# An encoder trunk on one core: the gates of two branches as seven block products ahead of attention, and two weight sums from adding transfers

## The chip, the cores and the metric

The kernel runs on one core of a Trainium2 chip. The metric is the device time of one execution in microseconds, as the median of several runs; lower is better. A profile of one execution gives, for each engine, which instruction ran when and what it waited for. The engines are PE (TensorE, the matrix engine; PEld is its loading of weights), DVE (VectorE), ACT (ScalarE), POOL (GpSimd) and SP (SyncE, which here issues transfers and computes nothing). Each engine works through its own list of instructions strictly in order.

## The reference

Two layers of an encoder on 512 tokens of width 1024, in float32. Cut to what matters:

```python
x = layer_norm(x, ln_in_g, ln_in_b)
for l in range(2):
    proj = x @ w_in[l]                       # 1024 -> 6816
    na_q, na_k, na_v, df_q, df_k, df_v, m_cq, m_ckv, m_kr, gate_pre = split(proj)
    na_out  = neighbourhood_attention(na_q, na_k, na_v, rpb)          # 8 heads of 64
    df_out  = diff_attention(df_q, df_k, df_v, lam, subln_g)          # 4 heads of 2 x 64
    mla_out = latent_attention(m_cq, m_ckv, m_kr, w_qb, w_kvb, ...)   # 8 heads
    gates   = sigmoid(gate_pre + b_gate[l])                           # 3 branches x 1024
    merged  = sum(gates[:, b] * (o_b @ w_branch[l, b]) for b, o_b in ((0, na_out), (1, df_out), (2, mla_out)))
    x = layer_norm(ALPHA * x + merged @ w_out[l], ln1)
    gu = x @ w_ffn_in[l]                     # 1024 -> 2 x 2816
    x = layer_norm(ALPHA * x + (silu(gu[:, :2816]) * gu[:, 2816:]) @ w_ffn_out[l], ln2)
```

A differential head has two score matrices, takes a softmax of each, mixes the two with the factor lam, multiplies by the values, and normalizes the result by its root mean square.

## The kernel before

**Precision and tiles.** Every float32 operand is held as two parts, a rounded one (hi) and the remainder (lo), both in a format that PE reads fast. A product is three matmuls: hi x hi, hi x lo, lo x hi (`mm3`, and in `gemm_w` and `gemm_x` lines 156 to 158). A weight tile is loaded into a slot and split by `wsplit`: ACT copies it into `whi` (L138), DVE subtracts (`wlo`, L139). The transposed input lies in `xth` and `xtl`, 8 blocks of 128 channels x 512 tokens. Other splits go through `split` (ACT in L221, DVE in L222; L224 and L225 with a scale).

**Memory.** `H` is a pool of 8 slots of 128 x 1024 float32, `R` one of 38 slots of 128 x 512 hi or lo values. Weight loads use two `raw` buffers and four each for `whi` and `wlo`. PSUM, where matmuls write, has two banks under each of the names `acc`, `sc`, `pv` and `tr`.

**A layer.** First the values of neighbourhood attention (`na_values`) and the latents (`latents`: 672 columns in two halves of 336, then norms and transposes). Then 4 pairs of heads of neighbourhood attention (`na_pair`), 4 pairs of latent attention (`mla_pair`), 4 differential heads (`df_proj`, `df_head`; L476 and L477 are its scores, L478 the maximum, L481 to L483 the mixing of the two softmaxes, L486 the transposes, L491 and L492 the values, L495 to L503 the norm and transposing of the result). The output projection and the FFN follow.

**Gates and merges.** A gate step, `gates(l, b, mp, ...)`, makes 256 channels of branch `b`'s gate: two products of 8 x 3 matmuls of 512 columns, and Tanh, since sigmoid(x) = (1 + tanh(x/2))/2. A merge step multiplies a branch's projected output by its gate and adds it up. Which of these steps are written after which head is a table, `PLAN`: rows 0 to 3 after the pairs of neighbourhood attention, rows 4 to 7 after those of latent attention, rows 8 to 11 after the differential heads, row 12 last. `G21g` is gate step `mp` = 1 of branch 2, put into buffers `gt`; with `h` it lies in a slot of `H`; `M21` is its merge. The program is written in that order, and a scheduler then orders each engine's instructions: it takes those that are ready by its own reckoning of time, so that the matmuls of gates and merges come to lie between those of the heads.

**Block products.** In the FFN two of 11 sets of 256 gate and 256 up columns are computed plainly, the other 9 by `ffn_fast`. It cuts the weights into four blocks (top and bottom half of the 1024 channels, gate and up columns) and the input into four (channel halves `kh`, token halves `th`), and gets the four results from seven products of blocks rather than eight, with sums of weight blocks and sums of input blocks (`x_sums`, once per layer, eight `R` slot pairs). One product (`product`, L784) is 24 matmuls of 256 columns. The weight sums are formed on DVE, in place in `H` slots (L844 to L846, and one later on g1); a set loads four blocks of 512 KB.

All transfers of weights, inputs and copies are issued on SP's queue, in order.

Of the kernel before, what the change touches and what calls it, by code (L numbers as in the profile page):

```python
# [16 lines left out]
D = 1024  # L17
# [19 lines left out]
    "G20h",  # L37
# [8 lines left out]
    "",  # L46
# [35 lines left out]
def trunk(ctx, tc, x, ln_in, w_in, feat, bias, lamv, w_mla, w_mlr, w_mlv, w_branch, w_out,  # L82
# [23 lines left out]
    xd = [xs.tile([128, D], F32, name=f"xd{t}") for t in range(NT)]  # L106

# [401 lines left out]
    def latents(l, g):  # L509
        lat = [H.get() for _ in range(NT)]  # L510
        krs = [i[:, 672:800] for i in lat]
        for i in krs:
            G.memset(i, 0.0)
        for hf in range(2):
            c0 = C_LAT + hf * 336
            src = lambda a, b: [w_in[l, a:b, c0:c0 + 336]]
            ch = wload_ks(src, 336, (3, 3, 2))
            for t in range(NT):
                p = bank("acc")[:, :336]
                gemm_x(p, ch, slice(0, 336), XT, tsl(t), KD)  # L520
                A.activation(lat[t][:, hf * 336:(hf + 1) * 336], p, AF.Copy)
        for t in range(NT):
            for a, b in ((0, 384), (384, 640)):
                ss = stat()
                sq = ptile()
                A.activation(sq[:, :b - a], lat[t][:, a:b], AF.Square, scale=(b - a) ** -0.5, accum_out=ss)
                rpow(ss, ss, RMS_EPS)
                V.tensor_scalar(lat[t][:, a:b], lat[t][:, a:b], ss, None, op0=OP.mult)
            t1 = sp.tile([128, 32], F32, tag="kr1", name="kr1", bufs=2)
            t2 = sp.tile([128, 32], F32, tag="kr2", name="kr2", bufs=2)  # L530
            kr = lat[t][:, 640:672]
            V.tensor_mul(t1, kr, cosm[:, t])
            V.tensor_mul(t2[:, 0:16], kr[:, 16:32], sinm[:, t, 0:16])
            V.tensor_mul(t2[:, 16:32], kr[:, 0:16], sinm[:, t, 16:32])
            V.tensor_add(krs[t][:, 32:64], t1, t2)
            V.tensor_copy(krs[t][:, 64:96], krs[t][:, 32:64])
# [201 lines left out]
    def x_sums():  # L738
# [5 lines left out]
        for i in range(2):  # L744
# [9 lines left out]
            V.tensor_sub(t1, q(h(0, 1)), q(h(0, 0)))  # L754
            V.tensor_sub(d, q(lo(0, 1)), q(lo(0, 0)))
            V.tensor_add(t1, t1, d)
            V.tensor_sub(t2, q(h(1, 1)), t1)
            V.tensor_add(t2, t2, q(lo(1, 1)))
            halves(1, ts[1])
            halves(0, ts[0])  # L760
            V.tensor_sub(d, t2, q(h(0, 0)))
            V.tensor_sub(d, d, q(lo(0, 0)))
            halves(2, ts[2])
            V.tensor_sub(t1, q(h(1, 0)), t2)
            V.tensor_add(t1, t1, q(lo(1, 0)))
# [21 lines left out]
    def hidden(gate, up):  # L787
# [3 lines left out]
        V.tensor_mul(sg, sg, up)  # L791
# [31 lines left out]
    def ffn_fast(l, m, sums):  # L823


        def load(t, base, kh):
            c = slice(base + m * 128, base + (m + 2) * 128)
            nc.sync.dma_start(t.rearrange("p (k c) -> p k c", k=4),
                              w_ffn_in[l, kh * 512:(kh + 1) * 512, c].rearrange("(k p) c -> p k c", p=128))
            return t  # L830
# [4 lines left out]
        g0, u0, u1 = load(H.get(), 0, 0), load(H.get(), D_FF, 0), load(H.get(), D_FF, 1)  # L835
        s = H.get()
        g1 = load(wp.tile([128, 1024], F32, tag="raw", name="raw", bufs=2), 0, 1)
# [4 lines left out]
        t1, t2, t3, t4 = sums  # L842
        with tc.high_priority():
            V.tensor_add(s, u0, u1)  # L844
            V.tensor_sub(u0, g0, u0)
            V.tensor_sub(g0, s, g0)  # L846
# [9 lines left out]
        with tc.high_priority():  # L856
            V.tensor_sub(g1, g1, g0)
# [4 lines left out]
        H.put(s, u0, g0, u1)  # L862
        res = [hidden(px, p1)]
        res.append(hidden(u2, u3))
        return res

# [23 lines left out]
    for l in range(DEPTH):  # L890
# [19 lines left out]
        tiles, cq, ckv, kr = latents(l, fp[:, 25:30])  # L910
# [3 lines left out]
        def fill(steps):  # L914

            for kind, b, mp, *place in steps:
                b, mp, place = int(b), int(mp), "".join(place)
                if kind == "G":
# [12 lines left out]
                    gates(l, b, mp, bg, gt)  # L931
# [165 lines left out]
```

## Time and profile before

| | |
|---|---|
| median of 3 runs | 1848.38 us (1847.4 to 1851.75) |
| the profiled execution | 1850.09 us, of which the profile's span is 1847.0 us |
| granted TensorE clock | 0.998 |
| PE busy | 1814.9 us, 98% of the span |
| DVE busy | 1309.9 us, 71% |
| ACT busy | 897.8 us, 49% |
| POOL busy | 90.1 us, 5% |
| read from memory | 177.24 MB; all transfers 106 GB/s on average |

The layers take about half of the span each. In layer 0 the values of neighbourhood attention end near 42 us, the differential heads lie at about 390 to 510 us, and the block products of the FFN begin near 640 us. Matmuls are pipelined: one is issued before the one ahead has ended, so the duration in a row is longer than the distance to the next start, and it is that distance (the pitch) that counts in a run of matmuls.

### The profile page before, as it was taken

Reading aid. Unit: us, or ns where it says so; the run is one execution under the profiler, and the core shown is the slowest. Engines: PE = TensorE matmul, PEld = TensorE weight load, DVE = VectorE, ACT = ScalarE, POOL = GpSimd, SP = SyncE. Lnnn points to the kernel's source line nnn. Section 1 sums busy time; section 2 is a strip of 40 time slices with the busy share of each in tenths; the row PEclk is TensorE's granted clock in tenths of the full one; section 3 lists DMA queues with packets and bytes.
Section 4 is the critical chain, followed back from the end, with each engine's and each line's share of the span. In section 5 each row is a group of like instructions: output and inputs, shape, how many; then the busy total and the mean of one; then the engine's idle time right before and its main releaser. Section 6 shows DMA issues by size and latency. Waiting matters only on the chain.

```text
span 1847.0 us, 28601 instructions
## 1 busy us (share of the span) xinstructions
PE 1814.9 (98%) x11248; PEld 1617.9 (88%) x11248; DVE 1309.9 (71%) x2204; ACT 897.8 (49%) x1612; POOL 90.1 (5%) x165
## 2 busy tenths in 40 slices
PE   7999999999999999999999999999999999999997
PEld 5988899988888999999789888999888799899996
DVE  6488887665568767777756888867655687676766
ACT  4567776555433433334336677755554234333331
POOL 4100000000001000000001000000000000000001
PEclk9999999999999999999999999999999999999999
DMA  7453232222262132323445332322233512323222
GB/s 258 116 164 95 89 94 75 83 78 86 85 201 81 58 114 81 117 89 103 151 123 170 112 98 87 92 63 87 75 98 103 182 58 94 113 92 108 93 98 80
DMA packets 167766, 195.86 MB, mean 106 GB/s; under 512 B 8529, under 2 KB 132689, under 8 KB 167633
## 3 DMA queue, kind: packets, MB, share of 16 engines
q1 hardware_dynamic: 167632, 194.05, 33.7%
q8 instruction: 88, 1.44, 0.3%
q14 instruction: 46, 0.37, 0.1%
HBM read 177.24 MB, written 9.44 MB: 101 GB/s over the span
## 4 chain that ended last, share of the span: by engine, by line
PE 89%; DVE 5%; DMA 3%; ACT 1%; issue 1%; SPq 0%; POOLq 0%; DVEq 0%; POOL 0%; ACTq 0%
PE acc L157 18%; PE acc L158 18%; PE acc L156 17%; PE sc L784 9%; PE pv L784 7%; DVE wlo L139 2%; PE tr L648 2%; PE sc L156 1%; DMA f<-in_w_ffn_in_dram 1%; PE sc L158 1%; PE sc L157 1%; PE pv L157 1%; PE pv L158 1%; PE pv L156 1%; PE pv L491 1%
## 5 line engine op out<-in xcount | busy, mean ns | idle before, releaser
L138 ACT ACTIVATE whi<-raw 128x1024 fp32r<-128x1024 f32 (+3 forms) x246 | 254.3, 1034 | 289.4 <-PE acc L157 54.1
L139 DVE TENSOR_TENSOR wlo<-raw,whi 128x1024 fp32r<-128x1024 f32 (+3 forms) x246 | 293.6, 1195 | 132.2 <-ACT whi L138 129.0
L156 PE MATMUL acc<-xth,whi 128*128 128x512 f32 x512 | 204.0, 399 | 0.3 <-ACT f L672 0.3
L158 PE MATMUL acc<-xth,wlo 128*128 128x512 f32 x512 | 202.7, 396 | 0.0
L157 PE MATMUL acc<-xtl,whi 128*128 128x512 f32 x512 | 202.6, 396 | 0.0
L138 ACT ACTIVATE whi<-f 128x1024 fp32r<-128x1024 f32 x90 | 94.6, 1057 | 182.4 <-PE acc L158 102.3
L157 PE MATMUL acc<-wlo,r 128*128 128x512 f32 (+1 forms) x440 | 171.3, 390 | 2.2 <-DVE wlo L139 2.2
L158 PE MATMUL acc<-whi,r 128*128 128x512 f32 (+1 forms) x440 | 170.7, 389 | 0.0
L156 PE MATMUL acc<-whi,r 128*128 128x512 f32 (+1 forms) x440 | 169.0, 390 | 0.6 <-ACT whi L138 0.5
L157 PE MATMUL acc<-wlo,xth 128*128 128x256 f32 (+2 forms) x544 | 162.4, 299 | 1.3 <-DVE wlo L139 1.3
L156 PE MATMUL acc<-whi,xth 128*128 128x256 f32 (+2 forms) x544 | 161.7, 299 | 1.7 <-ACT whi L138 1.6
L158 PE MATMUL acc<-whi,xtl 128*128 128x256 f32 (+2 forms) x544 | 162.2, 299 | 0.0
L784 PE MATMUL pv<-r,whi 128*128 128x256 f32 x864 | 156.0, 280 | 2.3 <-DVE P L853 2.0
L784 PEld LDWEIGHTS pv<-r,whi 128*128 128x128 f32 x864 | 132.3, 188 | 5.2 <-issue 2.8
L139 DVE TENSOR_TENSOR wlo<-f,whi 128x1024 fp32r<-128x1024 f32 x90 | 109.4, 1221 | 34.7 <-ACT whi L138 34.7
L784 PE MATMUL sc<-xth,whi 128*128 128x256 f32 x432 | 120.5, 279 | 0.0
L784 PE MATMUL pv<-r,wlo 128*128 128x256 f32 x432 | 120.5, 279 | 0.0
L784 PE MATMUL sc<-xtl,whi 128*128 128x256 f32 x432 | 120.3, 279 | 0.0
L784 PE MATMUL sc<-xth,wlo 128*128 128x256 f32 x432 | 119.9, 279 | 0.0
L156 PEld LDWEIGHTS acc<-xth,whi 128*128 128x128 f32 x512 | 96.3, 188 | 19.5 <-ACT f L672 0.7
L157 PEld LDWEIGHTS acc<-xtl,whi 128*128 128x128 f32 x512 | 96.4, 188 | 18.8
L158 PEld LDWEIGHTS acc<-xth,wlo 128*128 128x128 f32 x512 | 96.4, 188 | 18.7
(255 smaller groups left out, 4462.2 us busy)
## 6 DMA issues: line engine op xcount, KB each, us to landing
raw<-in_w_in_dram SPq DMA_DIRECT2D x64, 512.0 KB, 3.7
f<-in_w_ffn_in_dram SPq DMA_DIRECT2D x54, 512.0 KB, 3.7
raw<-in_w_ffn_out_dram SPq DMA_DIRECT2D x44, 512.0 KB, 3.7
raw<-in_w_ffn_in_dram SPq DMA_DIRECT2D x34, 512.0 KB, 3.5
raw<-in_w_in_dram SPq DMA_DIRECT2D x64, 256.0 KB, 3.3
raw<-in_w_branch_dram SPq DMA_DIRECT2D x24, 512.0 KB, 3.3
raw<-in_w_out_dram SPq DMA_DIRECT2D x16, 512.0 KB, 3.6
r<-r SPq DMA_DIRECT2D x56, 128.0 KB, 2.7
```

The lines of the kernel that those rows point to most:

```text
L138: A.activation(hi[:, :n], raw[:, :n], AF.Copy)
L139: V.tensor_sub(lo[:, :n], raw[:, :n], f32(hi[:, :n]))
L156: T.matmul(o, lh[0], rh[0], start=first, stop=False)
L157: T.matmul(o, lh[0], rh[1], start=False, stop=False)
L158: T.matmul(o, lh[1], rh[0], start=False, stop=last)
L491: T.matmul(po[:, 0:256], ch_[:, tsl(k)], v, start=k == 0, stop=False)
L648: T.transpose(pt[:, tsl(i)], prs[i % 2][:, tsl(kp + i // 2)], ident)
L784: T.matmul(o[:, c], w[a][:, j, f], x[e], start=fresh and mi == 0 and j == 0 and n == 0, stop=j == 3 and n == 2, skip_group_check=True)
```

## The change

It has two parts.

**Gates as block products.** The eight gate steps of branches 1 and 2 in each layer are not computed between the heads any longer. `ffn_fast` becomes `block_set`, which takes any weight matrix and two column groups of 256. `gates_fast` uses it for two gate steps at once (`mp` and `mp + 1`) and stores the Tanh results in eight new tensors `gd` in device memory. `latents` is cut in two, and its first part, `latent_rows`, calls `gates_fast` four times: ahead of the first half of the latents' columns, after each half, and at the end. `x_sums` runs there too, so twice per layer. Where `PLAN` has a `G` of branch 1 or 2, two reloads of 256 KB now stand. In `PLAN` the step `G20h` moves from row 0 to row 9. The four gate steps of branch 0 stay as they were.

**Weight sums by transfers.** In every block set, two of the four weight sums are now formed by transfers: s, the sum of the two halves of the second column group, and u0, the first half of the second group plus the first half of the first group. SP loads one block, and a second transfer, issued by POOL, adds the other block to it in place. A set so has seven loads of 512 KB, five on SP and two on POOL, and two additions of 128 x 1024 on DVE fewer. To make that possible with additions alone, signs are turned around: `x_sums` forms the negatives, and `hidden` multiplies by −1. The other two weight sums stay on DVE.

```diff
 PLAN = [i.split() for i in (
-    "G20h",
+    "",
...
-    "",
+    "G20h",
     "M20 G21g G22h M21 M22",
...
+    gd = {(b, mp): xs.tile([128, 1024], F32, name=f"gd{b}{mp}") for b in (1, 2) for mp in range(4)}
...
-    def latents(l, g):
+    def latent_rows(l, between):
         lat = [H.get() for _ in range(NT)]
+        between(0)
         for hf in range(2):
...
+            between(1 + hf)
+        between(3)
+        return lat
...
+            def less(o, a, b):
+                V.scalar_tensor_tensor(o, a, -1.0, b, op0=OP.mult, op1=OP.subtract)
+
-            V.tensor_sub(t1, q(h(0, 1)), q(h(0, 0)))
-            V.tensor_sub(d, q(lo(0, 1)), q(lo(0, 0)))
+            V.tensor_sub(t1, q(h(0, 0)), q(h(0, 1)))
+            V.tensor_sub(d, q(lo(0, 0)), q(lo(0, 1)))
...
-    def hidden(gate, up):
+    def hidden(gate, up, sign=1.0):
         sg = ptile()
         A.activation(sg, gate, AF.Silu)
-        V.tensor_mul(sg, sg, up)
+        V.scalar_tensor_tensor(sg, up, sign, sg, op0=OP.mult, op1=OP.mult)
...
-    def ffn_fast(l, m, sums):
+    def block_set(wsrc, top, bottom, sums):
+        t1, t2, t3, t4 = sums
+
+        def load(t, col, kh, add=False):
+            src = wsrc[kh * 512:(kh + 1) * 512, col:col + 256].rearrange("(k p) c -> p k c", p=128)
+            dst = t.rearrange("p (k c) -> p k c", k=4)
+            if add:
+                nc.gpsimd.dma_start(dst, src, accum_op=OP.add)
+            else:
+                nc.sync.dma_start(dst, src)
             return t
...
-        g0, u0, u1 = load(H.get(), 0, 0), load(H.get(), D_FF, 0), load(H.get(), D_FF, 1)
-        s = H.get()
-        g1 = load(wp.tile([128, 1024], F32, tag="raw", name="raw", bufs=2), 0, 1)
+        g0 = load(H.get(), top, 0)
+        s = load(load(H.get(), bottom, 0), bottom, 1, True)
+        u0 = load(load(H.get(), bottom, 0), top, 0, True)
+        u1 = load(H.get(), bottom, 1)
+        g1 = load(wp.tile([128, 1024], F32, tag="raw", name="raw", bufs=2), top, 1)
...
         with tc.high_priority():
-            V.tensor_add(s, u0, u1)
-            V.tensor_sub(u0, g0, u0)
-            V.tensor_sub(g0, s, g0)
+            V.tensor_add(g0, s, g0)
...
         with tc.high_priority():
-            V.tensor_sub(g1, g1, g0)
+            V.tensor_add(g1, g1, g0)
...
+        return (px, p1), (u2, u3)
+
+    def ffn_fast(l, m, sums):
+        return [hidden(*i, -1.0) for i in block_set(w_ffn_in[l], m * 128, D_FF + m * 128, sums)]
+
+    def gates_fast(l, b, mp, bg, sums):
+        col = C_GATE + b * D + mp * 256
+        for th, blocks in enumerate(block_set(w_in[l], col, col + 256, sums)):
+            for i, blk in enumerate(blocks):
+                t = ptile() if th == 0 and i == 0 else blk
+                for mi in range(2):
+                    m = b * 8 + 2 * (mp + i) + mi
+                    c = slice(mi * 256, mi * 256 + 256)
+                    A.activation(t[:, c], blk[:, c], AF.Tanh, bias=bg[:, m:m + 1], scale=(0.5, -0.5)[i])
+                dst = gd[b, mp + i].rearrange("p (m t) -> p m t", m=2)
+                nc.sync.dma_start(dst[:, :, th * 256:th * 256 + 256], t.rearrange("p (m t) -> p m t", m=2))
...
         vals = na_values(l, na_v, na_slots)
-        tiles, cq, ckv, kr = latents(l, fp[:, 25:30])
+        sums = x_sums()
+        lat = latent_rows(l, lambda i: gates_fast(l, 2 - i // 2, i % 2 * 2, bg, sums))
...
+        tiles, cq, ckv, kr = latents(l, fp[:, 25:30], lat)
...
                     if b:
                         held[b, mp] = pool, slot, gt
-                    gates(l, b, mp, bg, gt)
+                        for i in range(2):
+                            nc.sync.dma_start(gt[i], gd[b, mp][:, i * 512:(i + 1) * 512])
+                    else:
+                        gates(l, b, mp, bg, gt)
```

The change moves instructions on the engines at three places that matter below. In the rows that follow, a name is a tile and its number, an arrow points from the inputs to the output, and the last column is the shape.

On PE, late in the differential heads of layer 0, the list before stands like this; `acc_5021` belongs to a gate step, `sc` are scores, `pv` values, `tr` transposes:

```order
L157 MATMUL acc_5021<-xtl_73,whi_4985 128x512
L158 MATMUL acc_5021<-xth_72,wlo_4986 128x512
L476 MATMUL sc_4739<-r8_82,r27_101 128x512
L477 MATMUL sc_4739<-r9_83,r27_101 128x512
L156 MATMUL acc_5021<-xth_72,whi_4991 128x512
L491 MATMUL pv_4677<-r18_92,PP_4674 128x256
L157 MATMUL acc_5021<-xtl_73,whi_4991 128x512
L158 MATMUL acc_5021<-xth_72,wlo_4992 128x512
```

In the changed kernel the third differential head stands like this on PE (its lines have moved by one):

```order
L477 MATMUL sc_5058<-r30_104,r4_78 128x512
L478 MATMUL sc_5058<-r31_105,r4_78 128x512
L477 MATMUL sc_5063<-r32_106,r5_79 128x512
L478 MATMUL sc_5063<-r33_107,r5_79 128x512
L477 MATMUL sc_5097<-r30_104,r4_78 128x512
L478 MATMUL sc_5097<-r31_105,r4_78 128x512
L487 MATMUL tr_5032<-cons_120,P_5017 128x128 x4
L477 MATMUL sc_5102<-r32_106,r5_79 128x512
L478 MATMUL sc_5102<-r33_107,r5_79 128x512
L492 MATMUL pv_5040<-r34_108,PP_5037 128x256
```

Nothing but the head's own steps is left here: before, the gates' products stood between scores and values; now only 18 matmuls of a merge lie in the third and fourth head, and all other merges, projections and gates of branch 0 have come to lie further ahead.

On PE behind the values of neighbourhood attention in layer 0, the list before goes from the value product (`acc_368`) to the latents:

```order
L157 MATMUL acc_368<-wlo_278,xth_72 128x512
L158 MATMUL acc_368<-whi_277,xtl_73 128x512
L156 MATMUL acc_431<-whi_415,xth_72 128x336
L157 MATMUL acc_431<-wlo_416,xth_72 128x336
L158 MATMUL acc_431<-whi_415,xtl_73 128x336
```

In the changed kernel the first block set of gates stands there; `whi_468` is g0 itself, `whi_499` the sum g0 + s, `whi_529` the sum s, and `r14` to `r17` are input sums:

```order
L794 MATMUL sc_465<-xtl_73,whi_468 128x256
L794 MATMUL sc_465<-xth_72,wlo_469 128x256
L794 MATMUL pv_466<-r14_88,whi_499 128x256
L794 MATMUL pv_466<-r15_89,whi_499 128x256
L794 MATMUL sc_467<-r16_90,whi_529 128x256
L794 MATMUL sc_467<-r17_91,whi_529 128x256
L794 MATMUL pv_466<-r14_88,wlo_500 128x256
```

Three products of the set lie among one another, so PE comes to the weight sums right after the first product.

On DVE at the same place, the list before splits the latents' weights and the values' results:

```order
L222 TENSOR_TENSOR xtl_73<-tr_249,xth_72 128x4x128
L222 TENSOR_TENSOR r4_78<-acc_339,r4_78 128x2x128
L222 TENSOR_TENSOR r5_79<-acc_339,r5_79 128x2x128
L139 TENSOR_TENSOR wlo_416<-raw_413,whi_415 128x1008
L139 TENSOR_TENSOR wlo_422<-raw_419,whi_421 128x1008
```

In the changed kernel the input sums (L762 to L775) stand among the set's weights:

```order
L764 TENSOR_TENSOR gt_437<-xth_72 128x512
L140 TENSOR_TENSOR wlo_469<-f2_114,whi_468 128x1024
L223 TENSOR_TENSOR r19_93<-xs_419,r18_92 128x512
L223 TENSOR_TENSOR r21_95<-gt_417,r20_94 128x512
L223 TENSOR_TENSOR r6_80<-acc_376,r6_80 128x2x128
L765 TENSOR_TENSOR xs_439<-xtl_73 128x512
L862 TENSOR_TENSOR f2_114<-f3_115,f2_114 128x1024
L223 TENSOR_TENSOR r7_81<-acc_376,r7_81 128x2x128
L766 TENSOR_TENSOR gt_437<-gt_437,xs_439 128x512
L762 SCALAR_TENSOR_TENSOR gt_438<-xth_72,gt_437 128x512
L140 TENSOR_TENSOR wlo_500<-f2_114,whi_499 128x1024
```

The addition g0 + s (L862, `f2` is g0 and `f3` is s) has come to stand ahead of the second half of the input sums, so what follows on DVE is behind the transfer that completes s.

More of the change, by code (lines that the diff above doesn't have):

```diff
@@ L506, in df_head @@
         return o
-    def latents(l, g):
+    def latent_rows(l, between):
         lat = [H.get() for _ in range(NT)]
-        krs = [i[:, 672:800] for i in lat]
-        for i in krs:
-            G.memset(i, 0.0)
+        between(0)
         for hf in range(2):
@@ L521, in latents @@
                 A.activation(lat[t][:, hf * 336:(hf + 1) * 336], p, AF.Copy)
+            between(1 + hf)
+        between(3)
+        return lat
+    def latents(l, g, lat):
+        krs = [i[:, 672:800] for i in lat]
+        for i in krs:
+            G.memset(i, 0.0)
         for t in range(NT):
@@ L752, in halves @@
                 res[n].append(hl)
-            V.tensor_sub(t1, q(h(0, 1)), q(h(0, 0)))
-            V.tensor_sub(d, q(lo(0, 1)), q(lo(0, 0)))
+            def less(o, a, b):
+                V.scalar_tensor_tensor(o, a, -1.0, b, op0=OP.mult, op1=OP.subtract)
+            V.tensor_sub(t1, q(h(0, 0)), q(h(0, 1)))
+            V.tensor_sub(d, q(lo(0, 0)), q(lo(0, 1)))
             V.tensor_add(t1, t1, d)
-            V.tensor_sub(t2, q(h(1, 1)), t1)
-            V.tensor_add(t2, t2, q(lo(1, 1)))
+            less(t2, q(h(1, 1)), t1)
+            V.tensor_sub(t2, t2, q(lo(1, 1)))
             halves(1, ts[1])
             halves(0, ts[0])
-            V.tensor_sub(d, t2, q(h(0, 0)))
+            less(d, t2, q(h(0, 0)))
             V.tensor_sub(d, d, q(lo(0, 0)))
             halves(2, ts[2])
-            V.tensor_sub(t1, q(h(1, 0)), t2)
-            V.tensor_add(t1, t1, q(lo(1, 0)))
+            less(t1, q(h(1, 0)), t2)
+            V.tensor_sub(t1, t1, q(lo(1, 0)))
             halves(3, ts[0])
@@ L821, in ffn_plain @@
         return res
-    def ffn_fast(l, m, sums):
[L826 to L829, printed above, removed]
+    def block_set(wsrc, top, bottom, sums):
[7 more added lines that the diff above has]
+                nc.sync.dma_start(dst, src)
             return t
@@ L841, in ffn_fast @@
         A.activation(p1, px, AF.Copy)
-        t1, t2, t3, t4 = sums
         with tc.high_priority():
-            V.tensor_add(s, u0, u1)
-            V.tensor_sub(u0, g0, u0)
-            V.tensor_sub(g0, s, g0)
+            V.tensor_add(g0, s, g0)
         product(py, halved(g0), from_sum(t2), True)
@@ L861, in ffn_fast @@
         V.tensor_add(p1, py, p1)
[L862 to L865, printed above, removed]
+        H.put(g0, s, u0, u1)
+        return (px, p1), (u2, u3)
[12 more added lines that the diff above has]
+                nc.sync.dma_start(dst[:, :, th * 256:th * 256 + 256], t.rearrange("p (m t) -> p m t", m=2))
     def ffn_down(l, m0, sets, xt, first, hfs):
@@ L909, in trunk @@
         vals = na_values(l, na_v, na_slots)
-        tiles, cq, ckv, kr = latents(l, fp[:, 25:30])
+        sums = x_sums()
+        lat = latent_rows(l, lambda i: gates_fast(l, 2 - i // 2, i % 2 * 2, bg, sums))
+        for t in sums:
+            for hl in t:
+                R.put(*hl)
+        tiles, cq, ckv, kr = latents(l, fp[:, 25:30], lat)
         merged, held, outs = [], {}, [[], [], []]
```

## Prediction

> **What bounds the kernel now.** I read the page's head first: busy time, the 40 slices, the chain that ended last, and the transfers.
>
> ```profile
> span 1847.0 us, 28601 instructions
> PE 1814.9 (98%) x11248; PEld 1617.9 (88%) x11248; DVE 1309.9 (71%) x2204; ACT 897.8 (49%) x1612; POOL 90.1 (5%) x165
> PE   7999999999999999999999999999999999999997
> PEclk9999999999999999999999999999999999999999
> PE 89%; DVE 5%; DMA 3%; ACT 1%; issue 1%; SPq 0%; POOLq 0%; DVEq 0%; POOL 0%; ACTq 0%
> f<-in_w_ffn_in_dram SPq DMA_DIRECT2D x54, 512.0 KB, 3.7
> r<-r SPq DMA_DIRECT2D x56, 128.0 KB, 2.7
> ```
>
> TensorE is busy in 98% of the span, in every slice but the first and last, and carries 89% of the chain that ended last. VectorE has 71% on average. An average hides which stage could live without its filler, so I asked for busy time by windows: neighbourhood attention of layer 0, the program's start, the differential heads, the FFN's block products.
>
> ```profile
> 85.00:180.00 95.00, 94.70 (x524) 81.56 (x523) 78.76 (x227) 67.17 (x159) 0.00 (x0) 1.00 0.44 132
> 30.00:35.00 5.00, 5.00 (x24) 4.05 (x24) 2.20 (x5) 1.56 (x4) 0.08 (x1) 1.00 1.00 333
> 35.00:40.00 5.00, 5.00 (x23) 4.03 (x22) 2.19 (x4) 2.82 (x4) 0.00 (x0) 1.00 0.96 238
> 460.00:510.00 50.00, 50.00 (x247) 41.66 (x246) 26.84 (x49) 23.80 (x46) 3.62 (x8) 1.00 0.27 90
> 645.00:660.00 15.00, 15.00 (x128) 14.91 (x127) 13.45 (x14) 7.17 (x9) 0.00 (x0) 1.00 0.52 169
> ```
>
> The columns are the window, its length, busy us (and count) of PE, PEld, DVE, ACT and POOL, then granted clock, DMA share and GB/s. PE is full in all five. In the differential heads (460 to 510) it is full although VectorE works for only 26.84 of 50 us: the heads' chain of softmax steps is slow, and gate products lie in its gaps. In the FFN PE is full too, with VectorE at 13.45 of 15 us: making VectorE lighter there frees an engine that holds PE up almost nowhere. From 30 to 40 us the transfers are the full resource (share 1.00 and 0.96).
>
> So a gain has to be fewer or shorter matmuls, and a loss is any place where PE has too little of other work beside a chain.
>
> **T1: the gates' products, −20 us.** A gate is 48 matmuls of 512 columns; two gates as a block set are 168 of 256 columns.
>
> ```profile
> 20.03 0.39 PE L157 MATMUL acc<-wlo,xth 128*128 128x512 f32 x1
> 22.13 0.39 PE L157 MATMUL acc<-wlo,xth 128*128 128x512 f32 x1
> ...
> 488.44 0.39 PE L156 MATMUL acc<-xth,whi 128*128 128x512 f32 x1
> 491.88 0.39 PE L156 MATMUL acc<-xth,whi 128*128 128x512 f32 x1
> ...
> 640.07 0.28 PE L784 MATMUL sc<-xth,whi 128*128 128x256 f32 x1
> 642.89 0.28 PE L784 MATMUL sc<-xth,whi 128*128 128x256 f32 x1
> ```
>
> Matmuls overlap, so the price is the pitch. Nine pitches lie between the first two starts (0.233 us), fifteen between the next two (0.229), 24 between the last two (0.1175). The 16 moved gates took 16 x 48 x 0.229 to 0.233 = 176 to 179 us; 8 sets of 168 take 157.9. PE loses 18 to 21 us of work; I take 20.
>
> **T2: differential heads 2 and 3 without filler, +45 us.** In the order of the changed kernel the projections of heads 1 to 3 and all that is left of gates and merges are drawn ahead into heads 0 and 1. Heads 2 and 3 keep 18 foreign matmuls (18 x 0.233 = 4.2 us), where seven gates of about 11.1 us per layer stood. What they cost then is their own chain.
>
> ```profile
> 407.21 0.68 DVE L478 TENSOR_REDUCE ring<-sc 128x1 f32<-128x512 f32 x1
> 407.81 0.68 DVE L686 TENSOR_TENSOR f<-f,gt 128x512 f32<-128x512 f32 x1
> ...
> 426.03 0.69 DVE L478 TENSOR_REDUCE ring<-sc 128x1 f32<-128x512 f32 x1 [0.79 <-PE sc L477]
> 427.57 0.17 DVE L481 RECIPROCAL ring<-ring 128x2 f32<-128x2 f32 x1 [0.84 <-ACT P L479]
> 428.03 0.75 DVE L483 SCALAR_TENSOR_TENSOR P<-P,ring 128x512 f32<-128x512 f32 x1
> 436.08 0.35 DVE L495 SCALAR_TENSOR_TENSOR ost<-pv,ring,otmp 128x128 f32<-128x128 f32 x1 [1.32 <-ACT otmp L494]
> 437.86 0.29 DVE L499 TENSOR_SCALAR ost<-ost,ring 128x128 f32<-128x128 f32 x1 [1.43 <-POOL ring L232]
> ...
> 338.13 0.60 PE L486 MATMUL tr<-cons,P 128*128 128x128 f32 x4
> 338.49 0.36 PE L491 MATMUL pv<-r,PP 128*128 128x256 f32 x1
> 343.36 0.33 PE L491 MATMUL pv<-r,PP 128*128 128x256 f32 x1
> 343.82 0.33 PE L491 MATMUL pv<-r,PP 128*128 128x256 f32 x1
> ...
> 448.73 0.59 ACT L316 ACTIVATE r<-tr 64x512 fp32r<-64x512 f32 x1 [1.81 <-PE tr L462]
> 451.28 0.59 ACT L317 ACTIVATE r<-tr 64x512 fp32r<-64x512 f32 x1
> ...
> L221 ACT ACTIVATE PP<-tr 128x512 fp32r<-128x512 f32 x128 | 74.5, 596 | 31.4 <-PE tr L486 14.7 <-PE tr L648 8.5 <-PE tr L395 3.7
> L222 DVE TENSOR_TENSOR PP<-tr,PP 128x512 fp32r<-128x512 f32 x128 | 86.5, 684 | 12.1 <-ACT PP L221 11.3
> ```
>
> One query tile asks VectorE for two maxima (0.60 us apart), reciprocal and factor (0.46, from 427.57 to 428.03), the mix (0.75), the remainder of the split (0.68), the weighted output (0.35) and the scaling (0.29): with overlap about 3.5 us. After the last tile's scores comes a chain with nothing beside it: 2.00 from maximum to mix (426.03 to 428.03), 0.75, transposes 0.36 and hand-off, copy 0.60, remainder 0.68, values with their copy (ACT) 2.2, then 1.78 to the scaling (436.08 to 437.86), 0.29, and transposing and splitting the head's output about 1.2: 10 us.
>
> Head 3: three tiles x 3.5 + 10 = 20.5 us. PE's own work there is 16 scores x 0.233, 16 value pairs x 0.23 (343.36 to 343.82 is two) and 20 transposes x 0.09 (four in 0.36): 9.2. PE stands 11.3 us. Head 2: three tiles and the chain to its last values, 16.2; then head 3's operands, whose transposes stand behind it on PE: transposes 0.7, six ACT copies at 0.61, a remainder 0.7, the copy of the low half (2.7, the page's row r<-r) and hand-offs, 9 in all. Of these 25.2 us PE works 14.1, head 3's transposes and the 4.2 included: 11.1 idle. Per layer 22.4, for two layers 45. Low end, if only VectorE's stream counts (8 x 3.5 and 4 for operands, 32 against 23.3): 8.7 per layer, 17. High end, if hand-offs reach those on the quoted rows each time: 28 and 56. I take 45, since the chain is made of durations that stand in rows.
>
> **T3: neighbourhood attention, +4 us.** The gate that filled its first head pair (11.1 us) leaves. In the window of 95 us PE would keep 94.7 − 11.1 = 83.6 and VectorE 78.8 less about 2.4 for the gate's weight remainders. 76.4 of 84 is nine tenths, too close to fit without gaps; had VectorE gone through 95 us at its 83%, the whole 11 were lost. From 0 to 10; I take 4.
>
> **T4: entry into the new block sets, +12 us.** After the value product PE goes straight to the first set in layer 0, where latent and query-key products stood. The set needs its sums and its weights.
>
> ```profile
> 34.44 0.69 DVE L222 TENSOR_TENSOR xtl<-tr,xth 128x512 fp32r<-128x512 f32 x1 [2.59 <-ACT xth L221]
> 41.75 0.38 ACT L221 ACTIVATE r<-acc 128x256 fp32r<-128x256 f32 x1 [1.70 <-PE acc L158]
> L139 DVE TENSOR_TENSOR wlo<-f,whi 128x1024 fp32r<-128x1024 f32 x90 | 109.4, 1221 | 34.7 <-ACT whi L138 34.7
> L844 DVE TENSOR_TENSOR f<-f,f 128x1024 f32<-128x1024 f32 x18 | 22.1, 1225 | 14.9 <-DMA f<-in_w_ffn_in_dram 13.4 <-issue 1.2
> ```
>
> The transposed input is whole at 35.1, the value product ends near 41.7. The set's first weights lie in slots that xt held, free only when xt has been written out, and in SP's queue behind about 3.4 MB (the second weight sets, the latents' weights, two stores of 512 KB, the shift copies). At the 238 to 333 GB/s of the window that is 10 to 14 us after 34: near 45, with 1.2 + 1.1 for the split. The sum s lands, then its accumulating transfer on POOL's queue runs (no row of before has one; 3.7 us for the plain one), then an add and a split, 1.2 each: near 54, when the first product of 24 x 0.1175 = 2.8 us has long ended. About 9 us idle in layer 0 (0 to 18), 3 in layer 1, where the slots are free and the queue is short: 12. The rest lies in cover: four sets bring VectorE about 58 us of splits and adds and the 18 sums 12, beside 131 us of PE (values 22, sets 79, latents 30). If that cover were gone, the sums would end last.
>
> **T5: the clock after a gap, +4 us.**
>
> ```profile
> 15.10 0.63 PE L158 MATMUL acc<-whi,xtl 128*128 128x512 f32 x1
> 15.52 0.63 PE L156 MATMUL acc<-whi,xth 128*128 128x512 f32 x1
> ```
>
> The first products run at a pitch of 0.42 us, against 0.233 at 20 us, though the slices show full clock: after a stretch without work PE is slow for a while. After each of the gaps in T2 and T4 a microsecond of work may count nearly double: 0 to 20, I take 4. [...]
>
> **T6: FFN, −1 us.** Two adds of 1.2 us less per set on VectorE, 18 sets. PE waits there almost nowhere, so at most 5 us come back. In exchange s and u0 arrive as two transfers one behind the other. Each s is needed only after the first product, and most sets have 16.8 us of down-projection ahead, as cover; if the accumulation takes over 6 to 11 us, that is gone. +20 at the upper end. The stores and reloads of the gates (16 x 512 KB each) go out where the DMA share is 0.27 to 0.44, and hide.
>
> Sum: −20 + 45 + 4 + 12 + 4 − 1 = +44. The execution profiled took 1850.1 us (its span 1847.0), 1.7 above the median of 1848.4; 1848.4 + 44 = 1892.
>
> **Rivals.** *Cover holds: not slower.* The place is heads 2 and 3. If the chain hides within and across heads (next scores early, all four tiles in flight), only VectorE's stream is left, 8.7 us idle per layer or less, and T3 to T5 are near their low ends: 1848 − 20 + 9 to 17 = 1837 to 1845. For it: two banks each for scores and transposes let two tiles run at once. Against it: in PE's order head 3's operands stand behind head 2's values. It decides at 10 us of idle time per layer.
>
> *The accumulating transfer is slow.* 18 + 8 sets wait for s; where it comes later than the cover holds, PE stands for about 4 us, the plain transfer's time once more. On 9 to 24 of the sets that adds 36 to 96 us: 1928 to 1988. For it: nothing here shows one; against it: plain 512 KB in 3.7 us, on average a third of the DMA share in use. [...]
>
> *Slow clock inside the bare heads.* If PE, busy there for 9 of 20 us, works at the 0.42 pitch throughout, its own 23 us per layer become 42, part of it on the chain: about +9 per layer on top, 1910.
>
> **How the numbers follow.** The forecast has a chance of 0.65, the covered case 0.13 (half faster, half the same), slow transfers 0.10, slow clock 0.12. The range from 1858 to 1930 spans T2 from 22 to 56 with the ends of T3 to T5, the slow clock, and the beginning of slow transfers; it leaves out the covered case and most of the slow transfers. A measurement of this kernel tells about 0.3% (5.5 us) from no change: faster 0.07, same 0.06, slower 0.87.
>
> **What would show it.** T1: 256-wide matmuls at pitch 0.1175 in the sets ahead of attention. T2: windows over heads 2 and 3 with PE near 23 of 46 us, and waits for DVE and ACT in the chain that ended last; the same heads at 90% PE would make the prediction wrong. T3: PE below 94% in neighbourhood attention. T4: a gap on PE after the value product, ended by a split of a weight sum. T5: 512-wide pitches of 0.42 after gaps. T6: landing times of POOL's transfers; above 10 us the second rival holds.

## The result, and the profile after

The changed kernel takes 1953.2 us (1949.3 to 1958.4, 4 runs) against 1848.7: a ratio of 1.056, with an interval from 1.0535 to 1.0594. It is slower, as forecast, but by 104 us and not by 44. The profiled execution has a span of 1947.3 us, 100.3 more than before.

From the page of the changed kernel (engines, PE by slices, granted clock, chain, transfers):

```profile
span 1947.3 us, 30335 instructions
PE 1846.6 (95%) x11824; PEld 1650.2 (85%) x11824; DVE 1365.0 (70%) x2300; ACT 939.6 (48%) x1692; POOL 156.2 (8%) x217
PE   6899999999889999999999999999997999999998
PEclk9899999999889999999999999999998999999999
PE 74%; DVE 10%; DMA 7%; ACT 4%; issue 3%; POOL 0%; SPq 0%; DVEq 0%; POOLq 0%; ACTq 0%
q1 hardware_dynamic: 194672, 224.46, 37.6%
q0 software_dynamic: 27456, 27.27, 9.3%
f<-in_w_ffn_in_dram SPq DMA_DIRECT2D x72, 512.0 KB, 4.7
f<-in_w_ffn_in_dram POOLq DMA_DIRECT2D x36, 512.0 KB, 9.0
```

PE's part of the chain that ended last fell from 89% to 74%; VectorE, transfers and ACT took it. PE shows 31.7 us more busy time than before although its work became less: part of it ran at a lower clock. The row PEclk is below 9 in the second slice, in the 11th and 12th, where the heads of layer 0 are, and in the 31st, where those of layer 1 are. The mean granted clock is 0.977, against 0.998 before: 45 us of full clock were not granted in the span, against 4.

By windows (columns as above): the differential heads of layer 0 before, then of the changed kernel neighbourhood attention, the heads, the last two heads alone, and the entry into the gate sets (their first 40 us or so) in layers 0 and 1:

```profile
312.10:504.20 192.10, 192.10 (x1146) 169.03 (x1145) 116.61 (x206) 100.39 (x208) 14.83 (x32) 1.00 0.27 83
...
185.10:273.70 88.60, 85.57 (x476) 73.13 (x476) 74.70 (x225) 62.47 (x152) 0.00 (x0) 1.00 0.43 128
409.90:558.50 148.60, 132.34 (x817) 113.00 (x816) 98.74 (x193) 76.34 (x181) 15.53 (x32) 0.91 0.27 81
505.00:565.00 60.00, 44.06 (x175) 30.27 (x174) 40.03 (x86) 28.72 (x75) 7.42 (x16) 0.74 0.11 33
41.80:80.00 38.20, 26.21 (x151) 23.87 (x150) 22.95 (x29) 14.24 (x20) 3.84 (x3) 0.78 0.74 173
1000.00:1040.00 40.00, 33.92 (x193) 30.55 (x192) 32.15 (x48) 16.22 (x28) 3.63 (x3) 0.87 0.79 183
```

Seven gates (78 us of matmuls) left the heads, and the stage became only 43.5 us shorter. In the last two heads PE is busy for 44 of 60 us, at a granted clock of 0.74.

For a sum by stages I took, for each two matmuls that follow each other, the distance of their starts less the pitch of that shape at full clock (0.233 us for 512 columns, 0.1545 for 336, 0.1175 for 256, 0.09 for a transpose). What is left is time that PE lost, standing or slowed. Where a stage's border is drawn otherwise, an entry moves by up to 4 us. Both layers together, in us:

| kernel | start | sets and latents | neighbourhood | latent att. | diff. heads | rest | in all |
|---|---|---|---|---|---|---|---|
| before | 10.5 | 0.9 | 2.7 | 4.0 | 5.4 | 9.8 | 33 |
| changed | 12.4 | 32.9 | 11.2 | 11.3 | 70.0 | 17.8 | 156 |
| branch 1 back | 11.3 | 30.5 | 9.6 | 10.2 | 30.1 | 18.7 | 110 |
| all gates in both places | 10.0 | 34.0 | 2.7 | 5.4 | 5.5 | 18.8 | 76 |
| gate sets late | 10.5 | 19.0 | 12.5 | 5.9 | 70.2 | 21.6 | 140 |
| sums on VectorE | 10.6 | 28.1 | 12.1 | 10.9 | 68.1 | 9.6 | 139 |
| held to the keys | 11.8 | 37.2 | 10.7 | 10.7 | 84.8 | 21.8 | 177 |
| held to the last tile | 11.3 | 32.2 | 12.5 | 13.5 | 119.8 | 15.7 | 205 |
| the nearest | 10.8 | 11.1 | 14.0 | 11.0 | 29.7 | 12.7 | 89 |

The changed kernel loses 122 us more than before and has 21.3 less to do: 101, and the spans differ by 100.3. That these agree lies in how the count is made; what it tells is where the 122 are: 65 in the heads, 32 in the sets, 8 and 7 in the two other attentions, 8 in the rest, 2 at the start.

### The profile page after: what moved, and what is told of

Same layout as the page of the kernel before. It is cut to its first block, busy times and chain, and to the rows that moved or that the text cites. A ratio compares the mean times of both kernels' runs of the same rounds, so it can differ in the third digit from the quotient of the medians.

```text
span 1947.3 us, 30335 instructions
## 1 busy us (share of the span) xinstructions
PE 1846.6 (95%) x11824; PEld 1650.2 (85%) x11824; DVE 1365.0 (70%) x2300; ACT 939.6 (48%) x1692; POOL 156.2 (8%) x217
## 2 busy tenths in 40 slices
DMA packets 222270, 253.66 MB, mean 130 GB/s; under 512 B 10800, under 2 KB 183088, under 8 KB 222128
## 3 DMA queue, kind: packets, MB, share of 16 engines
q1 hardware_dynamic: 194672, 224.46, 37.6%
q0 software_dynamic: 27456, 27.27, 9.3%
## 4 chain that ended last, share of the span: by engine, by line
PE 74%; DVE 10%; DMA 7%; ACT 4%; issue 3%; POOL 0%; SPq 0%; DVEq 0%; POOLq 0%; ACTq 0%
PE sc L794 12%; PE acc L157 12%; PE acc L158 11%; PE acc L159 11%; PE pv L794 10%; DMA raw<-in_w_ffn_out_dram 2%; DVE wlo L140 2%; DMA raw<-in_w_in_dram 1%; PE tr L655 1%; ACT whi L139 1%; PE sc L158 1%; PE sc L159 1%; PE sc L157 1%; PE pv L158 1%; PE pv L159 1%
## 5 line engine op out<-in xcount | busy, mean ns | idle before, releaser
L139 ACT ACTIVATE whi<-raw 128x1024 fp32r<-128x1024 f32 (+5 forms) x230 | 237.1, 1032 | 320.5 <-DMA raw<-in_w_ffn_out_dram 69.9
L140 DVE TENSOR_TENSOR wlo<-raw,whi 128x1024 fp32r<-128x1024 f32 (+5 forms) x230 | 274.4, 1194 | 134.5 <-ACT whi L139 133.3
L794 PE MATMUL pv<-r,whi 128*128 128x256 f32 x1248 | 224.8, 280 | 7.8 <-ACT whi L139 4.9
L794 PEld LDWEIGHTS pv<-r,whi 128*128 128x128 f32 x1248 | 191.2, 189 | 9.8 <-ACT whi L139 5.2
L794 PEld LDWEIGHTS sc<-xth,whi 128*128 128x128 f32 x624 | 120.0, 192 | 9.6 <-ACT whi L139 6.0
L794 PEld LDWEIGHTS sc<-xth,wlo 128*128 128x128 f32 x624 | 120.0, 192 | 3.6 <-DVE wlo L140 2.7
L794 PEld LDWEIGHTS sc<-xtl,whi 128*128 128x128 f32 x624 | 120.1, 192 | 0.7
L794 PEld LDWEIGHTS pv<-r,wlo 128*128 128x128 f32 x624 | 117.6, 188 | 0.2 <-DVE wlo L140 0.2
L157 PEld LDWEIGHTS acc<-whi,xth 128*128 128x128 f32 x544 | 102.8, 189 | 8.2 <-ACT whi L139 5.5
L158 PEld LDWEIGHTS acc<-wlo,xth 128*128 128x128 f32 x544 | 103.0, 189 | 6.3 <-DVE wlo L140 3.6
```

The source lines that it names most:

```text
L139: A.activation(hi[:, :n], raw[:, :n], AF.Copy)
L140: V.tensor_sub(lo[:, :n], raw[:, :n], f32(hi[:, :n]))
L157: T.matmul(o, lh[0], rh[0], start=first, stop=False)
L158: T.matmul(o, lh[0], rh[1], start=False, stop=False)
L794: T.matmul(o[:, c], w[a][:, j, f], x[e], start=fresh and mi == 0 and j == 0 and n == 0, stop=j == 3 and n == 2, skip_group_check=True)
```

## The experiments

**The theory** after this: removing the gates took away the filler (other matmuls that PE does between the steps of a chain) of the heads and of the other attentions; the sets enter before their weights and sums are there; the lower clock (0.74 in the last two heads of layer 0, 0.78 at the entry into the sets) comes on top. **The rival**: the adding transfers, which take 9.0 us where a plain one takes 4.7 (3.7 before), hold up every set. By their share of the queues' time they cost twice as much per byte (9.3% for 27 MB against 37.6% for 224 MB). A second rival, for the heads: the amount of filler decides, not its place.

**The adding transfers alone** (ratio 1.0023, interval 1.0013 to 1.0032: 1853.1 us).

```diff
+        lat = latent_rows(l, lambda i: None)    # no sums, no gate sets here
+                    gates(l, b, mp, bg, gt)     # all b; PLAN as before
```

> Only the adding transfers are kept; all gates stay between the heads as before, and the input sums are formed once per layer. Theory of gaps and clock (the 100 us lie where the moved gates leave PE without work and where they enter, and the slowed clock after each gap doubles them): the FFN's sets have cover for the slower transfer, so 1848 us, from 1842 to 1856. Rival, the adding transfers (9.0 us to landing against 4.7 for a plain one, in 18 sets of the FFN): 2 to 4 us for each set, 1885 to 1920.

Its transfers into the weight slots, from its page:

```profile
f<-in_w_ffn_in_dram SPq DMA_DIRECT2D x72, 512.0 KB, 4.9
f<-in_w_ffn_in_dram POOLq DMA_DIRECT2D x36, 512.0 KB, 9.4
```

The adding transfer is as slow here, and the run is 4 us slower in all, as the theory had it. The FFN's cover is long enough; the rival falls as the main cause. The saving of 36 additions on VectorE bought nothing.

**All weight sums on VectorE, gates ahead** (1.0478, 1.0462 to 1.0494: 1937.7 us).

```diff
-        s = load(load(H.get(), bottom, 0), bottom, 1, True)
-        u0 = load(load(H.get(), bottom, 0), top, 0, True)
+        u0 = load(H.get(), bottom, 0)
+        s = H.get()
...
+            V.tensor_add(s, u0, u1)
+            V.tensor_add(u0, g0, u0)
```

> The gates stay ahead of attention as block sets; all four weight sums are formed on DVE again, with four plain loads per set. Theory of gaps and clock: the heads and neighbourhood attention keep their losses (about 67 and 18 us), only the entry into the sets gets shorter, by 5 to 15 us: 1938 to 1948. Rival, the adding transfers: most of the loss goes, 1850 to 1890.

15.5 us come back, half of them in the rest (17.8 to 9.6), 5 in the sets; the heads keep their 68. The total is the theory's, but the theory had it all at the sets' entry. So in the changed kernel the adding transfers are worth some 15 of the 104 us, although they cost 4 alone.

**The gate sets late** (1.0459, 1.0435 to 1.0483: 1934.6 us): `between(0)` to `between(3)` are called after both halves of the latents' columns.

> All four gate sets of a layer come after both halves of the latents' columns instead of ahead of, between and after them, so that some 30 us of other products stand before the first set. Theory of gaps and clock: the entry loses 34 us now, of which 20 to 30 go: 1923 to 1935. Rival, the adding transfers: each set still waits for its second transfer, and the time stays at 1945 to 1955. Second rival, VectorE late with the input sums: the gap moves behind the latents and stays half as long, 1935 to 1945.

18.6 us come back in all, at the border between the theory's range and the second rival's. The sets' loss falls from 33 to 19, by 14 where 20 to 30 were expected. A gap is left in layer 0, 6.8 us on the weights of the latents' first product, which now follows the values at once and so is the next to come too early. In the changed kernel itself the entry reads as follows (PE, ACT, POOL and DVE, layer 0):

```profile
46.18 1.06 ACT L139 ACTIVATE whi<-f 128x1024 fp32r<-128x1024 f32 x1 [7.83 <-DMA f<-in_w_in_dram]
47.29 0.58 PE L794 MATMUL sc<-xth,whi 128*128 128x256 f32 x1 [5.10 <-ACT whi L139]
50.02 1.29 POOL L844 DMA_DIRECT2D f<-in_w_in_dram  x1 [15.97 <-DVE r L223]
53.19 0.41 PE L794 MATMUL sc<-xth,wlo 128*128 128x256 f32 x1
56.13 1.23 DVE L862 TENSOR_TENSOR f<-f,f 128x1024 f32<-128x1024 f32 x1 [5.50 <-issue]
58.55 0.79 PE L794 MATMUL pv<-r,whi 128*128 128x256 f32 x2 [4.95 <-ACT whi L139]
```

g0 lands near 46, where the prediction had 45, and the sum s near 56, where it had 54; PE waits 5.1 and then 4.95 us. Between them the first product of 24 matmuls takes 5.9 us (47.29 to 53.19), twice the 2.8 at full clock. Since s comes only at 56, that slowness costs nothing, because PE would have waited for s anyway; slowness behind that point is not hidden so.

**The gates of branch 1 back between the heads** (1.0377, 1.0362 to 1.0393: 1919.5 us).

```diff
+        lat = latent_rows(l, lambda i: gates_fast(l, 2, i * 2, bg, sums) if i < 2 else None)
+                    if b == 2:      # reload; else gates(...) as before
```

> The four gate steps of branch 1 are computed between the heads again, as before; those of branch 2 stay in two block sets ahead of attention. Theory of gaps and clock: the heads' loss of 35 us per layer goes nearly whole, half of the saving on matmuls (10.6 us) is given back: 1953 - 67 + 11 = 1897, from 1888 to 1910. Rival, the adding transfers: two sets fewer per layer change little, 1940 to 1955.

Nearer to the theory than to the rival, and 10 us above the theory's range. The loss in the heads falls by 40, not by 67: four gates (45 us per layer) cover head 2, and head 3 stays bare (9 foreign matmuls in layer 0, against 196 in head 2), because they are drawn ahead once more.

**Idle matmuls, eight per tile ahead of the values** (1.0770, 1.0754 to 1.0787: 1990.4 us).

```diff
+            if h >= 2:
+                pw = bank("acc")
+                for k in range(8):
+                    T.matmul(pw, ch_[:, tsl(k % 4)], ch_, start=k == 0, stop=k == 7)
```

> The changed kernel with work added that does nothing: eight matmuls of 512 columns per query tile in differential heads 2 and 3, written to a bank that nobody reads, and dependent on the tile's own transposed probabilities, so that they run in the gaps. 128 matmuls, 30 us of PE's time at 0.233. Theory of gaps and clock: PE now loses in these heads 35 us per layer, about half of it by the clock; with the gaps smaller the clock stays up and the added work is free or better: 1925 to 1953. Rival, chain alone (the clock costs nothing, since the work that it slows lies beside the chain): 1953 to 1960. Rival, PE's own work is the limit there: 1953 + 30 = 1983.

A miss for the theory: +37 us, more than the 30 added. They need only the high half of the split, so they stand on PE ahead of the values, in the chain. The scheduler moved the real filler besides: in layer 0 head 1 keeps 54 foreign matmuls in place of 246, and heads 2 and 3 get 168 and 24 in place of 18 and none. The run doesn't tell what the clock costs.

**G00 and G01 earlier in the table** (1.0576, 1.0558 to 1.0594: 1955.3 us): `PLAN` row 0 is "G00h", row 3 "G01h", row 4 empty.

> The changed kernel with the gate steps of branch 0 earlier in the table: G00 after the first pair of neighbourhood attention and G01 after the fourth, which fills the place that G20 left. Theory of gaps and clock: neighbourhood attention loses 8 to 9 us per layer more than before; G00's 11 us fill most of that, and latent attention has other filler: 1953 - 12 to 17, so 1936 to 1943. Rival, the filler is only missing further on (zero sum): 1950 to 1956.

No gain, as the rival had it: by the same count neighbourhood attention loses 7 in place of 11 us, and latent attention 20 in place of 11. Filler moved from one stage was missed in the next.

**Merges held to the keys of heads 2 and 3** (1.0643, 1.0621 to 1.0666: 1966.3 us).

```diff
+            A.activation(hi[:, :n], raw[:, :n], AF.Copy, scale=1.0 if one is None else one)
...
+            V.tensor_scalar(one, f32(qk[1][1][0])[:, 0:1], 0.0, 1.0, op0=OP.mult, op1=OP.add)
```

> The changed kernel with the merges of branch 2 held back: the rounding of their weights is scaled by a one that is formed from the keys of differential head 2 (M20, M21) or 3 (M22, M23), so that these four merges (22 us of matmuls per layer) cannot be drawn ahead of that head. No work is added but four tiny instructions. Theory of gaps and clock: the loss in heads 2 and 3 (35 us per layer) falls to the last chain of head 3 and what head 1 now lacks, about 12: 1953 - 46 = 1907, from 1895 to 1925. Rival, the amount of filler is what is missing, not its place: the loss moves into heads 0 and 1, 1940 to 1955.

A plain miss, by 59 us, and above the rival's range too. The tiles of heads 2 and 3 now run with PE full, but the loss went into the passages: the last chain of one head and the operands of the next, for which nothing was ready any more.

**All remedies** (1.0524, 1.0509 to 1.0540: 1945.3 us), with the same way of holding (G03 and M03 to head 1 as well).

> All remedies at once: gate sets after the latents' columns, all weight sums on DVE, G00 and G01 earlier, and the gate G03 and the merges M03 and M20 to M23 held back to differential heads 1, 2 and 3. Theory of gaps and clock: 1953 - 19 - 15 - 13 - 50 = 1856, from 1842 to 1872; the saving of 20 us on the matmuls then shows beside what is left of the gaps. Rival, part of the remedies act on the same gap: 1875 to 1900.

Far above the theory's range and the rival's. The sets' loss falls to 14.5 us, the heads' rises to 85, where the same way of holding had missed before.

**Held to the last tile of the head before** (1.0834, 1.0807 to 1.0861: 2003.5 us).

```diff
+            if t == 3:
+                V.tensor_scalar(one, rl[:, 0:1], 0.0, 1.0, op0=OP.mult, op1=OP.add)
```

> Held back in another way: the one by which the weights are scaled is formed in the last query tile of a differential head, so G03 and M03 come free while head 0 ends, M20 while head 1 ends, M21 and M22 with head 2, M23 with head 3. The filler so falls into the passage from one head's end to the next head's scores, where PE stood still in the run that held them to the keys. No work is added. Theory of gaps, the passages are what is missing cover: the loss in the heads falls from 35 to about 25 us per layer (four tiles of 14 us of VectorE's stream against 7.4 of PE stay bare in each head): 1933, from 1920 to 1942. Rival, the amount of filler decides and not its place: 1948 to 1965.

The opposite of the forecast: 120 us lost in the heads. Merges and projections came together in the passages, where PE is now full (20.00 of 20 us from 430 to 450), and the tiles are bare in all heads.

**Idle matmuls behind the values** (1.0861, 1.0843 to 1.0879: 2007.8 us): four after each tile, twelve after the last, eight behind the queries.

> Idle matmuls as in the run with eight per tile, in heads 2 and 3, but written behind the values of each tile (four, and twelve after the last) and behind the queries (eight), so that they do not stand ahead of the values in the chain: 128 matmuls, 30 us. Theory of gaps: they fall into time in which PE stood still, and keep the clock up: 1945 to 1965. Rival, they are work in full, since PE's order is then late everywhere: 1980 to 1990.

Worse than either expected: the heads lose 98 us, since again projections moved. Adding work to test the clock failed twice, because it changes the order of everything else; what the clock alone costs stays open.

**All gates in both places** (1.1091, 1.1070 to 1.1113: 2050.8 us).

```diff
+                        gates(l, b, mp, bg, gt)      # b = 1, 2: computed again, then overwritten
                         for i in range(2):
                             nc.sync.dma_start(gt[i], gd[b, mp][:, i * 512:(i + 1) * 512])
```

> The block sets ahead of attention stay, and the 16 gate steps are also computed between the heads again, as before, and then overwritten by the reloads: all the filler is back, G20 in its old place. Theory of gaps: the losses in neighbourhood and latent attention and in the heads go, and the time is that of before plus the sets' 158 us, their entry (32) and the adding transfers (4 to 8): 2042 to 2050. Rival, the heads are slower for another reason (reloads, transfers): 1953 + 179 = 2132 less little.

1 us above the theory's range and 81 below the rival. With the filler back, the losses in the heads and in both other attentions are those of before (5.5, 2.7, 5.4), though the reloads and adding transfers are still there. What is left is the sets' entry and the rest. This settles the missing filler as the cause in those three stages, with the slower clock (0.91 over the heads of layer 0 in the changed kernel, 1.00 here) as a part of the loss that it brings.

**The nearest** (1.0251, 1.0233 to 1.0269: 1893.9 us): only branch 2 in sets, after the latents' columns, all sums on VectorE.

> What lost least so far, together: only branch 2 in block sets, these after the latents' columns, all weight sums on DVE. Theory of gaps, the remedies add up where they act in different places: 1919 - 19 - 15 = 1885, from 1878 to 1898. Rival, late sets and plain loads repair the same gap: 1898 to 1905.

Within the theory's range: the remedies add up where they act in different places. It is still 45 us slower than before, and no version here beats the kernel before.

The window over the differential heads of layer 0, in the runs with branch 1 back, held to the keys, held to the last tile, with idle matmuls behind the values, and with all gates in both places:

```profile
368.50:540.90 172.40, 164.41 (x1009) 143.70 (x1008) 108.87 (x201) 89.18 (x197) 14.69 (x32) 0.99 0.28 82
...
410.70:563.80 153.10, 130.48 (x816) 112.05 (x816) 99.67 (x197) 77.56 (x181) 14.89 (x32) 0.93 0.26 79
...
402.40:585.20 182.80, 153.93 (x868) 125.14 (x868) 110.03 (x205) 84.87 (x191) 20.50 (x32) 0.88 0.27 80
...
411.20:582.50 171.30, 147.75 (x857) 124.93 (x856) 97.55 (x189) 76.35 (x180) 15.32 (x32) 0.87 0.22 64
...
409.90:601.90 192.00, 192.00 (x1146) 168.92 (x1145) 116.57 (x206) 100.46 (x208) 14.83 (x32) 1.00 0.33 100
```

With all filler the stage takes 192.0 us and PE is full, exactly as before (192.1). With four of seven gates it takes 172.4, with none 148.6. The first 33 us of matmuls taken out gave 20 back, the next 45 gave 24. With no gates at all, the stage takes 148.6, 153.1 or 182.8 us by where its work lies (in the last, 51 more matmuls, some 12 us, have come into the window). So the amount of filler decides, as the second rival said, and place can make it worse; no place tried here made it better, and whether one exists stays open.

## Why the prediction was right or wrong

The sign and the place of the largest term were right; the sum was 60 us short. The step that failed most is T5, the clock. PE stood for 100.7 us of the span (1947.3 less 1846.6), against 32.1 before: 69 us more, where T2, T3, T4 and T6 together had 60. But its work, 21 us shorter, was busy for 32 us longer: 53 us, where T5 had 4. Not all of the 53 is the clock, since a matmul that stands alone is busy for longer than its pitch (one of 256 columns, alone at 1024.51 us, for 0.39 against 0.1175); 41 (45 less 4) is the full clock not granted beyond that of before. Most of that lies in four windows of the changed kernel: 15.6 us in the last two heads of layer 0, 12.0 in those of layer 1, 8.4 and 5.2 at the entry into the sets. The second of them, and a part of the first (columns as above):

```profile
1470.00:1520.00 50.00, 37.02 (x157) 25.97 (x158) 33.95 (x74) 26.41 (x70) 7.25 (x16) 0.76 0.06 19
529.00:545.00 16.00, 11.98 (x28) 7.08 (x29) 8.62 (x16) 7.57 (x17) 0.00 (x0) 0.50 0.17 50
```

These 41 us bound what the lower clock cost by this account; work slowed inside a wait costs nothing, and how much was of that kind stays open.

*T1 was right.* PE's rows in a gate set:

```profile
89.01 0.28 PE L794 MATMUL sc<-xth,whi 128*128 128x256 f32 x1
90.78 0.28 PE L794 MATMUL sc<-xth,whi 128*128 128x256 f32 x1
```

Fifteen pitches in 1.77 us, 0.118. The count by stages closes with a saving of 21.3, where 20 was taken.

*T2 named the place; its time without work held, its length did not.* What PE waited for in the heads of layer 0 of the changed kernel, total, times and longest:

```profile
PE tr L504 <- DVE ost L500: 5.0, 4, 2.4
PE sc L477 <- ACT P L480: 2.9, 3, 1.3
PE sc L478 <- DMA r<-r: 1.7, 3, 1.2
PE pv L493 <- DVE PP L223: 1.2, 3, 0.6
PE tr L487 <- DVE P L484: 1.0, 3, 0.6
```

These are links of the prediction's chain: the scaling at the head's end, the exponential, the copy of the low half, the remainder, the mix. Forecast 45, measured 65 with the slower clock in it. Of the 37 us that the count gives the heads of layer 0, 34 lie behind 505 us, in heads 2 and 3, as forecast. PE stood there for 15.9 of 60 us, less than the 22.4 of T2; but the two heads took some 52 us (505 to 557) where T2 had 46, and PE's 23 us of work came out as 44 of busy time.

*T5 was mis-sized.* It had 4 us for the clock in all. PE's rows at the end of head 3 and just behind it:

```profile
559.30 0.63 PE L158 MATMUL acc<-r,whi 128*128 128x512 f32 x1
560.15 0.63 PE L158 MATMUL acc<-r,whi 128*128 128x512 f32 x1
...
563.05 0.40 PE L158 MATMUL acc<-r,whi 128*128 128x512 f32 x1
563.75 0.39 PE L158 MATMUL acc<-r,whi 128*128 128x512 f32 x1
```

0.425 us per matmul, then 0.233. The prediction counted a microsecond of slow work behind each gap. Instead the clock is down for about half of the two heads (0.74 on average from 505 to 565), in one stretch for 16 us (0.50 from 529 to 545) while PE is busy for 12 of them. No wait there is long: PE's longest in the heads of layer 0 is the 2.4 us above. 0.09 of 148.6 us of clock were not granted over the heads of layer 0, 13 us; how much of that lay on the chain was not separated. That was the third rival, at 0.12, and it came together with the forecast, not in place of it: T2's 45 and the rival's 9 per layer make 63, near the 65. This is in part luck, since PE stood for less and was slowed for more than the two had it. At the end of head 3 PE works almost steadily from 558.3 on, and the slow pitch goes on to 562.6, 4.3 us at a granted clock of 0.50.

*T3 was counted for one layer, and the next stage left out.* Its working is of layer 0's window, and its 4 us stand once in the sum; 8.5 came for two layers in neighbourhood attention, about 4 in each, so the size held. PE's busy share there is 97% (85.57 of 88.60), above the 94% that was to be its sign. The other 7 came in latent attention, which the prediction put at nothing. It looked at the stage that lost its filler and not at the next: filler drawn ahead is missing later. In the run with the sets late latent attention lost only 5.9; why the sets' place matters there was not followed up.

*T4 had the mechanism of layer 0, not of layer 1.* Its waits and landing times were met within 2 us: 9 us were forecast, and the two waits are 10.1. But layer 0 lost 20, of which up to 8.4 are the clock (0.78 over 38.2 us). In layer 1 it had 3 us on the ground that queue and slots were free; 12 were lost. There PE waits for the splits of the input sums (1.5 and 1.0 us) and for ACT's copy of the first product (2.1), up to 5.2 us are the clock (0.87 over 40 us), and VectorE's in-order list holds the last layer norm behind the weight sum:

```profile
996.53 1.23 DVE L862 TENSOR_TENSOR f<-f,f 128x1024 f32<-128x1024 f32 x1 [4.46 <-DMA f<-in_w_in_dram]
997.67 1.41 DVE L254 SCALAR_TENSOR_TENSOR f<-f,ring,f 128x512 f32<-128x512 f32 x2
```

The addition waits 4.46 us for s, and the norm (L254), on which the transposed input depends, stands behind it. Since plain loads did not cure layer 1's loss (12 to 11 us) while later sets did (12 to 4), the early place of the sets is the cause, not this wait alone.

*T6 had the sign wrong.* −1 was forecast, +4 measured alone, and 15.5 came back when the adding transfers left the changed kernel. The rival of slow transfers was right about the transfer (9.0 us) and wrong about its price (36 to 96 us), since the FFN's cover mostly held.

*The range* failed by adding one likely value for each term while all terms that depend on bare time fell to the same side: heads +20, entry and start +22, other attentions +12, the rest +9, less the 4 us that T5 had. The slower clock is in the first two of these (0.91 over the heads of layer 0, 0.78 and 0.87 at the entries into the sets), so it should have been added to both.

## What to carry to other kernels

Where one engine is full all the time, work that it does between the steps of a slow chain is paid for once and hides the chain once: before moving it or making it cheaper, find the shortest time of the chain without it. Here 78 us of filler per layer bought back only 44. Where such filler was short, the slower clock (0.91 over the heads of layer 0, 0.78 at the entry into the sets) and VectorE's order (4.46 us in front of one sum) added to the loss in the same places, so the errors of the single terms didn't cancel; and an experiment that adds or holds work under a scheduler moves the rest too, so read its stages before its total.

## What the runs showed of the hardware

A transfer that adds to its target, issued by POOL, took twice as long as a plain one of the same size in the same slots, issued by SP (9.0 against 4.7 us in the changed kernel, 9.4 against 4.9 with the adding transfers alone), and about twice the queue time per byte (9.3% for 27.27 MB against 37.6% for 224.46 MB, and 6.7% for 18.88 MB against 35.9% for 203.49 MB); whether the adding or the other queue makes it slower was not separated. Plain loads of the FFN's blocks landed more slowly in these two kernels (4.7 and 4.9 us, against 3.7 before); they also move more bytes (253.66 and 224.20 MB, against 195.86).

PE's granted clock was at half for 16 us on end while PE was busy for 12 of them (0.50 from 529 to 545 in the changed kernel); PE's longest wait in these heads was 2.4 us.
